# Order on VectorE, larger output-projection chunks, a second issuer for the first weights, and another pace for attention's fill

## The chip, the cores and the metric

The kernel runs on one core of one Trainium2 chip, as one launch. The metric is device time in microseconds (us), the median of several runs. Five engines work side by side, each with its own queue of instructions: TensorE (PE; its weight loads are shown apart as PEld), VectorE (DVE), ScalarE (ACT), GpSimd (POOL) and SyncE (SP), which here issues nearly all DMAs. An instruction waits at the head of its engine's queue until its inputs and its buffer are there, and everything behind it waits too.

## The reference

One transformer block in float32 on 512 tokens with 1024 features, then a last norm (`reference`, cut):

```
x = x + 0.5 * swiglu(rmsnorm(x, norm_ffn1), w_gate1, w_up1, w_down1)     # 1024 -> 2816 -> 1024
x = x + hybrid_mixer(rmsnorm(x, norm_mix), w_in, ..., w_out, rel_bias)
x = x + 0.5 * swiglu(rmsnorm(x, norm_ffn2), w_gate2, w_up2, w_down2)
return rmsnorm(x, norm_final)
# hybrid_mixer: 8 "moba" heads (0 to 7) and 8 "nsa" heads (8 to 15) of 64 features;
# an nsa head sums three gated attentions: compressed keys, selected keys (ks), window keys (kw);
# the heads' outputs, side by side, are multiplied by w_out (1024 x 1024).
```

## The kernel before

**Precision.** Every float32 operand of a matmul is split into a high and a low half (`hi` by ScalarE, `lo = v - hi` by VectorE, or by GpSimd for weights during attention). A product is then three matmuls (`mm3`, L99 to L102): hi by hi, hi by lo, lo by hi. A matmul with 512 columns moves one 128x128 block against all tokens.

**Stages.** x lies transposed as eight blocks `xs[0..7]` of 128 features by 512 tokens. The stages are: loading x and the first weights (L110 to L121); the first feed-forward layer; the mixer (projections, attention, output projection); the second feed-forward layer; the last norm.

**Feed-forward (class `Ffn`).** The first four of the 22 blocks of hidden features are computed plainly (`plain`): a gate step and an up step each load a 512 KB chunk of weights and run 24 matmuls of 512 columns. The other eighteen are computed in pairs (`pair`) by a scheme with seven products in place of eight: a pair has 14 steps (seven products, each for gate and for up) of 12 matmuls of 256 columns. Four of the seven products, S1 to S4, take sums of weight blocks, which `sums` (L298 to L303) makes in place on VectorE, 144 in all; `halves_of` (L305 to L311) then splits a block into `sph` and `spl` with `halves_of_x` (L225). The weight blocks lie in 16 buffers `aw`, eight to a pair, and a later pair's DMA waits until its buffers are free. `down` multiplies by the down projection and adds to xs (L487). Between the plain steps and the first pairs, `sums_of_x` and `blocks_of_x` make the moving operands of the pairs on VectorE.

**What sets the order.** `go` (L424) writes the steps out in program order: at step i it emits loads for step i+12, sums for step i+6, splits for step i+4, the products of step i, and the evictions of step i-1. A planner then orders each engine's queue at compile time by its own estimate of times: an instruction whose inputs it takes to be ready may go ahead of one that stands earlier in the program. `tc.issue_after(ins)` keeps the instructions of its block, on the engine of `ins`, behind `ins`; `tc.high_priority()` moves some ahead. On the chip the order within a queue is fixed.

**Attention and its fill.** Attention (L1006 to L1032) is a list of steps: 52 for the nsa heads (13 for each of four pairs of heads), then 24 for the moba heads. A step is three parts, `logits` (matmuls, softmax), `turn` (transposes) and `values`. Between them runs the fill: jobs of `stream` (L780), each with a chunk of weights loaded and split three jobs ahead. The fill's jobs are, in order, the projections for the kw keys and for the next heads (24 matmuls of 512 columns, eight units of three), and parts of the output projection `w_out` (L766), whose jobs wait until the heads that they read are done (`out_done`). `target(i)` (L1021) says how many units are to have run at step i: 1.4 for each nsa step, 0.6 for each moba step. `need` runs fill at once when a step needs its result, and what is left runs after the last step.

**Output projection.** 32 jobs: for each of the eight output blocks d and each two of the eight input blocks k, a 128 KB DMA, two splits of 128x256, six matmuls into one of two PSUM banks `mm`, and an addition to xs[d] (L774). The jobs for k = 2, 3 (heads 4 to 7) come last; after each of them xs[d] is multiplied by the next norm's gain and split (`gained`, L143) and its squares are added up (`squares`, L157). A head's output is split in `out_halves` (L806): the last step adds two parts into `lo` on GpSimd (L823).

Of the kernel before, what the change touches and what calls it, by code (L numbers as in the profile page):

```python
# [29 lines left out]
def block_kernel(ctx: ExitStack, tc: tile.TileContext, A: dict, out: bass.AP):  # L30
# [81 lines left out]
    first_w = [chunk((8, 128)) for _ in range(2)]  # L112
    for k in range(NK):
        x = xp.tile([128, S], F32, name=f"x{k}")
        nc.sync.dma_start(x, A["xT"][k * 128:(k + 1) * 128])
        xs.append(x)
        if k == 0:
            nc.sync.dma_start(gcol, A["gcol"])
        if k < 4:
            i, h = k % 2, slice(4 * (k // 2), 4 * (k // 2) + 4)  # L120
            nc.sync.dma_start(first_w[i][:, h], A[("wg1", "wu1")[i]][0][:, h])  # L121
# [65 lines left out]
    class Ffn:  # L187
# [14 lines left out]
        def __init__(self, wg, wu, which, tmp, hp, sp):  # L202
            self.w, self.which, self.tmp, self.hp, self.sp = (wg, wu), which, tmp, hp, sp
            self.xg, self.hs, self.steps = None, {}, []
            self.b, self.temps = {}, {}
            self.behind_rms = None
# [18 lines left out]
        def halves_of_x(self, hi, lo, v):  # L225
            nc.scalar.activation(hi, v, AF.Copy)  # L226
            nc.vector.tensor_tensor(lo, v, f32(hi), ALU.subtract)  # L227
# [61 lines left out]
        def pair(self, f):  # L289
# [8 lines left out]
            def sums(m, name):  # L298
# [4 lines left out]
                nc.vector.tensor_tensor(to, x, y, op)  # L303
# [65 lines left out]
        def down(self, w, fs, then, tag="mm", groups=(1,) * NK):  # L369
# [9 lines left out]
            def halves_of(d):  # L379
                if d % (4 // n) == 0:  # L380
                    i = d * n % 8
                    for k, v in enumerate(halves(raw[d * n // 8][:, i:i + 4])):
# [72 lines left out]
    def bias_rows(hp):  # L455
# [5 lines left out]
        nc.sync.dma_start(tabs[0:32, :], A["rel_bias"])  # L461
        nc.sync.dma_start(far, A["rel_bias"][31:32, :].to_broadcast([32, 16]))
        rows = hp.tile([16, RVW], F32, name="rows", tag="h", bufs=16)
        parts = []
        for src, h0, c, m in ((A["oh_t"], 0, 0, RVW), (A["oh_c"], 8, 0, S), (A["oh_c"], 8, S, S)):
            oh = hp.tile([33, S], F32, name="oh", tag="h", bufs=16)
            nc.sync.dma_start(oh[:, :m], src[:, c:c + m])
# [83 lines left out]
    with ExitStack() as ph:  # L551
# [214 lines left out]
        def w_out(d, k0, k1):  # L766
            def body(w):
                while any(2 * k + 1 not in out_done for k in range(k0, k1)):
                    yield
                p = pt("mm", "pw")  # L770
                for k in range(k0, k1):
                    mm3(p, w[k - k0], oT[k], k == k0, k == k1 - 1)
                    yield
                nc.vector.tensor_tensor(xs[d], p, xs[d], ALU.add)  # L774
                if k1 == 4:
                    got["x", d] = gained(d, 2)
                    squares(tmp, d, "t", 6)
            return A["w_o"][d][:, k0:k1], body
# [27 lines left out]
        def out_halves(h):  # L806
# [16 lines left out]
            nc.gpsimd.tensor_tensor(lo[b], t[b], u[b], ALU.add)  # L823
# [146 lines left out]
        for i in range(4):  # L970
            fill += [proj(2 * i, moba_t("q", i)), proj(2 * i + 1, moba_t("k", i))]
            if i == 2:
                fill += [w_out(d, 4, 6) for d in range(NK)]
        fill += [w_out(d, k, k + 2) for k in (6, 0) for d in range(NK)]
        last = [w_out(d, 2, 4) for d in range(NK)]
# [45 lines left out]
        def target(i):  # L1021
            if i < n_nsa:
                return 1.4 * i
# [118 lines left out]
def _laid_out(x, norm_ffn1, w_ffn1_gate, w_ffn1_up, w_ffn1_down, norm_mix, w_in, cmp_pos_k, cmp_w1_k,  # L1142
# [22 lines left out]
        "w_o": _blocks(w_out[0], D, 128),  # L1165
# [29 lines left out]
```

## Time and profile before

| | us |
|---|---|
| median of three runs | 1010.56 |
| the three runs | 1010.56, 1012.22, 1008.08 |
| the profiled execution, device time | 1011.25 |
| its span, first to last instruction | 1009.5 |

| engine | busy us | share of the span |
|---|---|---|
| PE | 983.8 | 97% |
| PEld | 871.0 | 86% |
| DVE | 776.9 | 77% |
| ACT | 564.9 | 56% |
| POOL | 137.3 | 14% |

The span is one profiled execution; device time is the span and what lies around it (1.75 us). Matmuls are pipelined: the next one starts before the shown end of the one before, so the shares of PE count a little more than its work. The moment at which a matmul starts, and the idle time ahead of it, are exact enough to be read.

By time, the first feed-forward layer lies at 0 to about 400 us, the projections at 400 to 440, attention with its fill at 440 to 636, the end of the output projection at 636 to 654, the second feed-forward layer from 648 to the end.

### The profile page before, as it was taken

To read this page: it belongs to the slowest core of one execution; us is meant where nothing else is said; L and a number is where in the kernel's file an instruction comes from. 1 tells how busy PE (TensorE), PEld (TensorE's weight loads), DVE (VectorE), ACT (ScalarE), POOL (GpSimd) and SP (SyncE) were. 2 spreads that over 40 slices of the span, in tenths; PEclk is the share of its full clock that TensorE was granted. 3 is DMA by queue.
4 is the path that set the end of the run, shared out by engine and by line. 5 is a ranking of instruction groups with operands and counts; after the bars stand their busy time and mean duration, and the time that the engine had idled before them with its cause. 6 is when DMAs were issued, how large, how long until landed. Compare 5 with 4: busy or idle time off the path is not lost.

```text
span 1009.5 us, 17013 instructions
## 1 busy us (share of the span) xinstructions
PE 983.8 (97%) x6080; PEld 871.0 (86%) x6080; DVE 776.9 (77%) x1578; ACT 564.9 (56%) x1181; POOL 137.3 (14%) x193
## 2 busy tenths in 40 slices
PE   8999999999999999999999999999999999999996
PEld 6779999999999898787878888788899999999995
DVE  6797888788766488758888978779878888776744
ACT  6463654454444266557677977655455445444436
POOL 0000000000000000036555776300000000000002
PEclk9999999999999999999999999999999999999998
DMA  7254544233501125541011322425244232341102
GB/s 244 87 197 153 186 149 113 98 101 89 161 25 54 45 85 177 165 127 38 20 45 32 93 65 84 140 86 209 69 144 142 86 105 91 120 146 43 33 11 84
DMA packets 53513, 104.53 MB, mean 104 GB/s; under 512 B 10513, under 2 KB 19170, under 8 KB 53428
## 3 DMA queue, kind: packets, MB, share of 16 engines
q1 hardware_dynamic: 53428, 103.44, 32.6%
q8 instruction: 48, 0.79, 0.3%
q14 instruction: 37, 0.30, 0.1%
HBM read 97.98 MB, written 5.30 MB: 102 GB/s over the span
## 4 chain that ended last, share of the span: by engine, by line
PE 82%; DVE 11%; DMA 3%; issue 2%; ACT 1%; POOL 0%; SPq 0%; DVEq 0%; ACTq 0%; POOLq 0%
PE pd L102 6%; PE pd L100 6%; PE pd L101 6%; PE pu L100 6%; PE pu L102 5%; PE pu L101 5%; PE pw L100 4%; PE pw L101 4%; PE pw L102 4%; PE pp L102 3%; PE pgu L100 3%; PE pp L100 3%; PE pp L101 3%; PE pgu L101 3%; PE pv L100 3%; PE pgu L102 3%
## 5 line engine op out<-in xcount | busy, mean ns | idle before, releaser
L226 ACT ACTIVATE sph<-aw 128x512 fp32r<-128x512 f32 x252 | 155.7, 628 | 138.0 <-PE pu L101 68.1
L91 ACT ACTIVATE whi<-raw 128x512 fp32r<-128x512 f32 (+2 forms) x216 | 124.6, 589 | 151.3 <-PE pd L101 71.8
L227 DVE TENSOR_TENSOR spl<-aw,sph 128x512 fp32r<-128x512 f32 x252 | 170.0, 685 | 49.5 <-ACT sph L226 47.9
L101 PE MATMUL pd<-h,whi 128*128 128x512 f32 x336 | 131.9, 392 | 1.4 <-DVE h L255 1.4
L102 PE MATMUL pd<-h,wlo 128*128 128x512 f32 x336 | 130.9, 390 | 0.8 <-DVE wlo L95 0.6
L95 DVE TENSOR_TENSOR wlo<-raw,whi 128x512 fp32r<-128x512 f32 (+1 forms) x168 | 110.9, 671 | 23.9 <-ACT whi L91 22.6
L100 PE MATMUL pd<-h,whi 128*128 128x512 f32 x336 | 129.0, 392 | 0.0
L100 PE MATMUL pu<-th,sph 128*128 128x256 f32 x432 | 121.5, 281 | 1.1 <-DVE t L339 1.1
L303 DVE TENSOR_TENSOR aw<-aw 128x512 f32<-128x512 f32 x144 | 97.6, 683 | 31.7 <-DMA aw<-in_wg 13.6
L102 PE MATMUL pu<-th,spl 128*128 128x256 f32 x432 | 121.1, 280 | 0.0
L101 PE MATMUL pu<-tl,sph 128*128 128x256 f32 x432 | 121.0, 280 | 0.0
L487 DVE SCALAR_TENSOR_TENSOR x<-pd,x 128x512 f32<-128x512 f32 x88 | 59.9, 685 | 44.7 <-PE pd L102 44.4
L100 PEld LDWEIGHTS pu<-th,sph 128*128 128x128 f32 x432 | 81.6, 189 | 2.8 <-DVE t L339 1.3
L101 PEld LDWEIGHTS pu<-tl,sph 128*128 128x128 f32 x432 | 81.9, 190 | 1.1
L100 PE MATMUL pw<-xo,sph 128*128 128x256 f32 x288 | 80.8, 281 | 0.8 <-DVE x L487 0.5
L102 PEld LDWEIGHTS pu<-th,spl 128*128 128x128 f32 x432 | 81.2, 188 | 0.1
L101 PE MATMUL pw<-xo,sph 128*128 128x256 f32 x288 | 80.4, 280 | 0.0
L102 PE MATMUL pw<-xo,spl 128*128 128x256 f32 x288 | 79.7, 280 | 0.0
L102 PEld LDWEIGHTS pd<-h,wlo 128*128 128x128 f32 x336 | 63.1, 188 | 14.1 <-DVE wlo L95 1.2
L101 PEld LDWEIGHTS pd<-h,whi 128*128 128x128 f32 x336 | 63.3, 188 | 12.8 <-DVE h L255 2.2
L100 PEld LDWEIGHTS pd<-h,whi 128*128 128x128 f32 x336 | 62.9, 188 | 11.1
L100 PEld LDWEIGHTS pw<-xo,sph 128*128 128x128 f32 x288 | 54.1, 188 | 2.6 <-ACT sph L226 1.6
(245 smaller groups left out, 2454.5 us busy)
## 6 DMA issues: line engine op xcount, KB each, us to landing
aw<-in_wg SPq DMA_DIRECT2D x72, 256.0 KB, 3.8
aw<-in_wu SPq DMA_DIRECT2D x72, 256.0 KB, 3.6
raw<-in_wd1a SPq DMA_DIRECT2D x20, 512.0 KB, 4.7
raw<-in_wd2a SPq DMA_DIRECT2D x20, 512.0 KB, 4.8
raw<-in_w_a SPq DMA_DIRECT2D x16, 512.0 KB, 4.4
raw<-in_w SPq DMA_DIRECT2D x8, 512.0 KB, 3.7
raw<-in_w_o SPq DMA_DIRECT2D x32, 128.0 KB, 2.2
raw<-in_wg SPq DMA_DIRECT2D x7, 512.0 KB, 3.8
```

Of the source, the lines that this page charges most:

```text
L91: nc.scalar.activation(hi, v, AF.Copy)
L95: nc.vector.tensor_tensor(lo, v, f32(hi), ALU.subtract)
L100: nc.tensor.matmul(p, w[0], v[0], start=first, stop=False, skip_group_check=again)
L101: nc.tensor.matmul(p, w[0], v[1], start=False, stop=False, skip_group_check=again)
L102: nc.tensor.matmul(p, w[1], v[0], start=False, stop=last, skip_group_check=again)
L226: nc.scalar.activation(hi, v, AF.Copy)
L227: nc.vector.tensor_tensor(lo, v, f32(hi), ALU.subtract)
L303: nc.vector.tensor_tensor(to, x, y, op)
L487: nc.vector.scalar_tensor_tensor(xs[d], p, 0.5, xs[d], ALU.mult, ALU.add)
```

## The change

It makes six edits. (1) Each sum of weights, and each split of down-projection weights, is kept on VectorE behind the newest `lo` of `halves_of_x` that the program has written so far (`behind_lo`). (2) The first gate weights are issued by ScalarE as two halves ahead of x; the first up weights come from SyncE as one DMA behind x; the small loads for the bias are kept behind them. (3) The output projection has eight jobs of four output blocks and two input blocks, a 512 KB DMA each; the last two jobs run k outside and the four blocks inside, in four banks (two `mm`, two `s`). (4) `lo` of head 7 is added on VectorE. (5) `target` begins at 8 and rises by 1.4 - 8/52 = 1.246 for each nsa step, with the same value at step 52. (6) The layout of w_out in memory follows (3).

```diff
     first_w = [chunk((8, 128)) for _ in range(2)]
+    for h in (slice(0, 4), slice(4, 8)):
+        nc.scalar.dma_start(first_w[0][:, h], A["wg1"][0][:, h])
     for k in range(NK):
         x = xp.tile([128, S], F32, name=f"x{k}")
         nc.sync.dma_start(x, A["xT"][k * 128:(k + 1) * 128])
         xs.append(x)
         if k == 0:
             nc.sync.dma_start(gcol, A["gcol"])
-        if k < 4:
-            i, h = k % 2, slice(4 * (k // 2), 4 * (k // 2) + 4)
-            nc.sync.dma_start(first_w[i][:, h], A[("wg1", "wu1")[i]][0][:, h])
+    fetch(first_w[1], A["wu1"][0])
...
         def halves_of_x(self, hi, lo, v):
             nc.scalar.activation(hi, v, AF.Copy)
-            nc.vector.tensor_tensor(lo, v, f32(hi), ALU.subtract)
+            self.last_lo = nc.vector.tensor_tensor(lo, v, f32(hi), ALU.subtract)
+
+        def behind_lo(self):
+
+            return tc.issue_after(self.last_lo.ins) if self.last_lo else nullcontext()
...
-                nc.vector.tensor_tensor(to, x, y, op)
+                with self.behind_lo():
+                    nc.vector.tensor_tensor(to, x, y, op)
...
-                    for k, v in enumerate(halves(raw[d * n // 8][:, i:i + 4])):
+                    with self.behind_lo():
+                        parts = halves(raw[d * n // 8][:, i:i + 4])
+                    for k, v in enumerate(parts):
                         got[d + k // n, k % n] = v
...
-        nc.sync.dma_start(tabs[0:32, :], A["rel_bias"])
-        nc.sync.dma_start(far, A["rel_bias"][31:32, :].to_broadcast([32, 16]))
+        with behind_fetched():
+            nc.sync.dma_start(tabs[0:32, :], A["rel_bias"])
+            nc.sync.dma_start(far, A["rel_bias"][31:32, :].to_broadcast([32, 16]))
...
-        def w_out(d, k0, k1):
+        def w_out(g, k0, last=False):
+
             def body(w):
-                while any(2 * k + 1 not in out_done for k in range(k0, k1)):
+                while any(2 * k + 1 not in out_done for k in (k0, k0 + 1)):
                     yield
-                p = pt("mm", "pw")
-                for k in range(k0, k1):
-                    mm3(p, w[k - k0], oT[k], k == k0, k == k1 - 1)
+                ps = {}
+                for i, k in [(i, k) for k in range(2) for i in range(4)] if last else [
+                        (i, k) for i in range(4) for k in range(2)]:
+                    if k == 0:
+                        ps[i] = pt("mm" if not last or i < 2 else "s", "pw")
+                    mm3(ps[i], w[2 * i + k], oT[k0 + k], k == 0, k == 1)
                     yield
-                nc.vector.tensor_tensor(xs[d], p, xs[d], ALU.add)
-                if k1 == 4:
-                    got["x", d] = gained(d, 2)
-                    squares(tmp, d, "t", 6)
-            return A["w_o"][d][:, k0:k1], body
+                    if k == 1:
+                        d = 4 * g + i
+                        nc.vector.tensor_tensor(xs[d], ps[i], xs[d], ALU.add)
+                        if last:
+                            got["x", d] = gained(d, 2)
+                            squares(tmp, d, "t", 6)
+            return A["w_o"][k0 // 2, g], body
...
-            nc.gpsimd.tensor_tensor(lo[b], t[b], u[b], ALU.add)
+
+            (nc.vector if h == 7 else nc.gpsimd).tensor_tensor(lo[b], t[b], u[b], ALU.add)
...
-                fill += [w_out(d, 4, 6) for d in range(NK)]
-        fill += [w_out(d, k, k + 2) for k in (6, 0) for d in range(NK)]
-        last = [w_out(d, 2, 4) for d in range(NK)]
+                fill += [w_out(g, 4) for g in range(2)]
+        fill += [w_out(g, k) for k in (6, 0) for g in range(2)]
+        last = [w_out(g, 2, True) for g in range(2)]
...
         def target(i):
             if i < n_nsa:
-                return 1.4 * i
+                return 8 + (1.4 - 8 / n_nsa) * i
             return 1.4 * n_nsa + 0.6 * (i - n_nsa)
```

## Rows read from the trace of the kernel before

**Rows 1.** Page, busy us of each engine, share of the span, instructions
```profile
PE 983.8 (97%) x6080; PEld 871.0 (86%) x6080; DVE 776.9 (77%) x1578; ACT 564.9 (56%) x1181; POOL 137.3 (14%) x193
```

**Rows 2.** Windows: stretch, length, busy us (instructions) by engine, granted clock, DMA, GB/s
```profile
48.00:104.00 56.00, 53.37 (x315) 46.38 (x314) 50.94 (x96) 28.33 (x59) 0.00 (x0) 1.00 0.49 170
690.00:765.00 75.00, 72.33 (x487) 65.58 (x486) 63.99 (x118) 40.96 (x84) 0.00 (x0) 1.00 0.40 135
104.00:400.00 296.00, 295.61 (x2007) 273.32 (x2006) 223.25 (x395) 150.99 (x294) 1.41 (x5) 1.00 0.34 105
...
457.00:478.00 21.00, 18.56 (x116) 14.75 (x115) 17.99 (x71) 16.27 (x47) 11.31 (x18) 1.00 0.13 37
504.00:518.00 14.00, 13.32 (x87) 10.55 (x85) 11.00 (x36) 11.78 (x31) 7.98 (x12) 1.00 0.07 19
636.00:650.00 14.00, 11.60 (x50) 8.61 (x50) 10.41 (x16) 10.49 (x20) 4.28 (x5) 1.00 0.51 160
```

**Rows 3.** Timeline of SP, ACT and PE at 0 to 7: start, us, work [idle <-releaser]
```profile
1.65 0.43 SPq L121 DMA_DIRECT2D raw<-in_wg  x1
...
3.76 0.72 ACT L147 ACTIVATE xo<-x,gcol 128x512 fp32r<-128x512 f32 x1 [1.53 <-DMA gcol<-in_gcol]
5.71 0.63 ACT L91 ACTIVATE whi<-raw 128x512 fp32r<-128x512 f32 x1 [1.23 <-DMA raw<-in_wg]
...
6.39 0.79 PE L100 MATMUL pgu<-xo,whi 128*128 128x512 f32 x1 [1.15 <-ACT whi L91]
```

**Rows 4.** Windows of the start, columns as in rows 2
```profile
6.40:11.00 4.60, 4.60 (x10) 2.85 (x11) 3.19 (x5) 3.24 (x6) 0.00 (x0) 1.00 0.99 338
11.00:25.00 14.00, 14.00 (x63) 11.57 (x62) 12.48 (x21) 10.48 (x19) 0.00 (x0) 1.00 0.75 238
```

**Rows 5.** Timeline of DVE: three moments at 61 to 97, one at 757
```profile
61.20 0.67 DVE L303 TENSOR_TENSOR aw<-aw 128x512 f32<-128x512 f32 x1
...
67.96 0.67 DVE L255 TENSOR_TENSOR h<-t,h 128x512 fp32r<-128x512 f32 x1
...
96.14 0.69 DVE L303 TENSOR_TENSOR aw<-aw 128x512 f32<-128x512 f32 x1 [1.88 <-DMA aw<-in_wg]
...
757.16 0.69 DVE L303 TENSOR_TENSOR aw<-aw 128x512 f32<-128x512 f32 x1 [4.23 <-DMA aw<-in_wg]
```

**Rows 6.** Windows of the projections' tile pp alone: PE, PEld, DVE
```profile
457.00:478.00 21.00, 0.24 (x2) 0.31 (x3) 0.67 (x1) 1.00 0.13 37
478.00:504.00 26.00, 17.99 (x72) 12.98 (x70) 1.28 (x2) 1.00 0.06 17
```

**Rows 7.** Waits of PE at 430 to 660: us in total, times, longest
```profile
PE pw L101 <- POOL kvn L823: 1.6, 1, 1.6
...
PE pw L100 <- DVE x L774: 0.8, 2, 0.5
```

**Rows 8.** Timeline of DVE and POOL at the end of the output projection
```profile
637.01 0.68 DVE L820 TENSOR_TENSOR to<-po,kvn 64x512 f32<-64x512 f32 x1 [0.41 <-POOL wlo L93]
...
638.46 1.26 POOL L823 TENSOR_TENSOR kvn<-to,u 64x512 fp32r<-64x512 f32 x1 [1.49 <-ACT u L822]
...
649.01 0.74 DVE L148 SCALAR_TENSOR_TENSOR xo<-x,gcol,xo 128x512 fp32r<-128x512 f32 x1
649.67 0.68 DVE L774 TENSOR_TENSOR x<-pw,x 128x512 f32<-128x512 f32 x1
650.27 0.67 DVE L164 TENSOR_TENSOR acc<-acc,sq 128x512 f32<-128x512 f32 x1
```

**Rows 9.** Groups by shape at 430 to 660: count, busy us, mean ns, idle before
```profile
L91 ACT ACTIVATE whi<-raw 128x512 fp32r<-128x512 f32 x27 | 16.9, 627 | 10.7 <-PE pp L101 6.4 <-issue 1.8 <-ACT th L891 0.8
L91 ACT ACTIVATE whi<-raw 128x256 fp32r<-128x256 f32 x32 | 13.2, 414 | 12.6 <-PE pw L101 7.0 <-PE pp L101 3.8 <-POOL kvn L823 0.9
L93 POOL TENSOR_TENSOR wlo<-raw,whi 128x256 fp32r<-128x256 f32 x32 | 24.8, 780 | 10.6 <-ACT whi L91 9.1 <-PE pw L101 1.1
L93 POOL TENSOR_TENSOR wlo<-raw,whi 128x512 fp32r<-128x512 f32 x16 | 21.2, 1324 | 4.0 <-ACT whi L91 4.0
```

More of the change, by code (lines that the diff above doesn't have):

```diff
@@ L205, in __init__ @@
             self.b, self.temps = {}, {}
+            self.last_lo = None
             self.behind_rms = None
@@ L466, in bias_rows @@
             oh = hp.tile([33, S], F32, name="oh", tag="h", bufs=16)
-            nc.sync.dma_start(oh[:, :m], src[:, c:c + m])
+            with behind_fetched():
+                nc.sync.dma_start(oh[:, :m], src[:, c:c + m])
             parts.append((oh, h0, c, m))
@@ L1164, in _laid_out @@
         "pos": c(cat([pos, pos], axis=0)),
-        "w_o": _blocks(w_out[0], D, 128),
+        "w_o": c(w_out[0].reshape(4, 2, 128, 2, 4, 128).transpose(0, 3, 2, 4, 1, 5)).reshape(4, 2, 128, 8, 128),
         "wg2": _blocks(w_ffn2_gate[0], D, 128), "wu2": _blocks(w_ffn2_up[0], D, 128),
```

## The prediction

> **What bounds the kernel now.** I read the page first. TensorE is busy for 983.8 of 1009.5 us, 97% [rows 1], and the change takes no matmul away and adds none: the same products of the output projection come in another order. So the ceiling on any gain is TensorE's idle time, 1009.5 - 983.8 = 25.7 us, and each edit can win only what lies idle where it acts. That is why I read the windows next, stretch by stretch. The long stretches of pairs are full: at 104 to 400 TensorE idles for 296.00 - 295.61 = 0.39 us [rows 2]. The idle time that the edits can reach lies in short places: the change from plain steps to pairs in each feed-forward layer (56.00 - 53.37 = 2.63 at 48 to 104, 75.00 - 72.33 = 2.67 at 690 to 765), attention's stretches without fill (2.44 at 457 to 478, 0.68 at 504 to 518, and one more of 0.65 like it at 535 to 548), and the end of the output projection (14.00 - 11.60 = 2.40 at 636 to 650) [rows 2]; to these comes the start, where the first product waits 1.15 us [rows 3]. Together 12.6 us. The waits and the timelines then say what ended each. (The profiled execution took 1011.25 us, its span 1009.5 and 1.75 around it; the median of the runs is 1010.56. I take the sum off the median; off the profiled execution it would come 0.7 later. A difference under 0.5%, 5.05 us, counts as no change, so faster means under 1005.5 and slower over 1015.6.)
>
> **The change, part by part.**
>
> *First weights by ScalarE.* ScalarE splits x's first block at 3.76, when the gains have landed, then sits idle for 1.23 us until the first half of the gate's weights lands, splits it in 0.63 at 5.71, and the first product starts at 6.39 [rows 3]. The weights were third in SyncE's queue, issued at 1.65. Issued by ScalarE at the outset, they are there when x is: split of x to 3.76 + 0.72 = 4.48, split of the weights to 5.11, so the first product at about 5.25, when the eight warming matmuls end (6.39 less its idle 1.15). That is 1.1 earlier. The trace has no DMA issued by ScalarE; SyncE's took 0.43, so two take 0.86 ahead of a ScalarE that idles 1.53 before 3.76 [rows 3]: hidden at that price, and up to 0.76 each. What is late next: the up weights now come behind x, as the last 512 KB. With the DMA engines 99% busy at 338 GB/s [rows 4], these two 256 KB take 2 x 0.78 = 1.6 us. The first products run at 4.60/10 = 0.46 us each, later ones at 14.00/63 = 0.222, both with a granted clock of 1.00 [rows 4]; 24 gate products from 5.25, the slow pace held to 11, last until about 13.5, and the up weights should be split about 0.2 later. I take -0.9. Bounds: -1.6, if the fast pace comes earlier too, and +1.6, if the up weights keep TensorE waiting for their whole landing.
> The Trainium skill (DMA: Bandwidth & Descriptors, "Issuing engines are not separate DMA queues") says that DMAs from ScalarE and SyncE share the same 16 engines, and a second issuer saves the issue time alone. Taken alone it makes this edit worth the two issues, 0.86 instead of 0.9, so nothing hangs on it here. The 99% of [rows 4] agrees that the engines, not the issuer, are then the limit.
>
> *Sums behind the newest lo.* At 48 to 104 VectorE is busy for 50.94 of 56.00 [rows 2]. Sums for the coming pairs go ahead of work needed sooner: the first at 61.20, three more before `h` at 67.96 [rows 5], which TensorE's down products wait for. At 96.14 a sum sat 1.88 us at the head of the queue until its DMA landed, with an eviction behind it that TensorE needed; at 757.16 another sat 4.23 [rows 5]. Held behind the newest `lo`, four sums of 0.67 leave the path of `h` (2.7 us), so the early half of these stalls should go; what is late next is the sums themselves, in a stretch where VectorE has only 5 us free. A sum that waits for its DMA is not cured by order: its buffer came free late, so its stall shrinks only as far as the splits before it come earlier. I take 60% of 2.63 + 2.67 = 5.30: -3.2. Bounds: -5.3 (all of it) and +3 (the four sums now hold a product back instead). In the long stretches the 144 sums gain nothing, with 0.39 us idle; what they could lose is a rival below. Splits of down weights under the same rule: nothing, since a down step's weights are split four steps ahead of their use, and a step is 12 products at 295.61/2007 = 0.147 us [rows 2], 1.8 us.
>
> *Attention's fill.* At 457 to 478 two matmuls of projections ran, at 478 to 504 seventy-two [rows 6]; in the first stretch VectorE is busy for 17.99 of 21.00 and TensorE idles for 2.44 [rows 2]. Before, 18.2 units (1.4 x 13) are due at the end of the first pair of heads; after, 8 + 1.246 x 13 = 24.2. Six units, 18 matmuls x 0.222 = 4.0 us, move into that stretch, from work that otherwise runs where TensorE is full. They can fill 2.44 at most, for the chain through VectorE needs TensorE at moments of its own: I take -2.0. Each later pair gets 1.246 x 13 = 16.2 units instead of 18.2, and the stretches with 0.68 and 0.65 idle stay. Bounds: -2.4, and +2.7: four units (8 less the 4.2 due at step 3) are put ahead of the first heads and push their chain back by 12 x 0.222.
>
> *Output projection in fours, and head 7 on VectorE.* TensorE's one long wait after attention is 1.6 us for `lo` of the last head [rows 7], which GpSimd made in 1.26 from 638.46 [rows 8]. Now the last job runs k = 2 for four blocks first, 12 products x 0.222 = 2.7 us that need no head but the earlier ones, and the addition takes about 0.68 on VectorE (a row of the same shape [rows 8]) in place of 1.26. The wait is gone: -1.6. Two waits for a bank, 0.8 together [rows 7], meet four banks in place of two: -0.5. Against it: four evictions now come within 3 x 0.67 us, each with 0.68 + 0.74 + 0.67 = 2.1 us of VectorE behind it [rows 8]. If VectorE takes them strictly in turn, the fourth bank is free 3 x 2.1 + 0.7 = 7.0 us after the first block is done, and TensorE wants it after 2 x 3 x 0.67 = 4.0: a stall of 3.0, which products of the next layer can cover, as far as they are planned there. I take -2.1; bounds -2.4 and +0.9. The splits: 32 of 128x256 become 16 of 128x512, so ScalarE saves 13.2 - 16 x 0.627 = 3.2 us and GpSimd 24.8 - 16 x 1.324 = 3.6 [rows 9]; neither ends a wait of TensorE here, so zero. A chunk's split is longer (1.32 for 0.78), but it is covered by the 24 products, 5.3 us, of the chunk before it. SyncE issues eight DMAs for 32: zero, the queue stands waiting for buffers.
>
> The sum: -0.9 - 3.2 - 2.0 - 2.1 = -8.2, so 1010.56 - 8.2 = **1002.4 us**. The bounds add up to -11.7 and +8.2, 998.9 to 1018.8; that all lie at one end is unlikely. The planner lays out every queue anew, so a wait can also vanish or appear elsewhere, a few us either way; and TensorE's pace loses time that the idle column does not count. For both I let the low end go to 995.
>
> **The rivals.**
> *A. Only the certain parts hold.* VectorE bounds the change to pairs whatever the order, and the fill finds no idle moment. Then the start and the end are left: -0.9 - 2.1 = -3.0, 1007.6, no change. For it: VectorE is busy for 91% of 48 to 104. Against: at 690 to 765 it has 11.0 us free [rows 2].
> *B. Sums come late in every pair; slower.* A sum behind a `lo` that waits for ScalarE or a buffer can itself be late for its product. Place: the products S1 to S4 of eighteen pairs, 144 of them. Price: at 0.1 us each 14.4; with the other parts, -5.0, it gives 1010.56 - 5.0 + 14.4 = 1020. It decides from (5.05 + 5.0)/144 = 0.07 us a sum on. For it: TensorE has no slack there. Against: the order that is forced is about that of the program, where a sum stands two steps (3.5 us) ahead of its split and six ahead of its product, and VectorE has 296.00 - 223.25 = 72.8 us free at 104 to 400 [rows 2].
> *C. The fill moves the stall.* Eight units ahead push the heads' chain by 2.7 us, and thinner fill later opens the 0.68 and 0.65 by as much again as they are: -0.9 - 3.2 - 2.1 + 2.7 + 1.3 = -2.2, 1008.4, no change. For it: the stretch at 457 to 478 is VectorE's. Against: VectorE idles ahead of it, so the chain can start later at no cost.
>
> **How the numbers follow.** Forecast 0.58, A 0.18, C 0.12, B 0.12. The forecast's own range is 997 to 1006; nearly all of it, 0.55, and some of A and C, 0.07, are faster by over 0.5%: 0.62. Slower: most of B, 0.10, and a rest of the others, 0.01: 0.11. Within 0.5%: 0.27. The range 995 to 1012 leaves out B and a thin low end.
>
> **What would show it.** Start: the first `pgu` product near 5.25. Sums: no `aw` sum on VectorE between 61 and 68 ahead of `h`, and TensorE's idle time in the two changes to pairs down from 5.3 to about 2. Fill: matmuls of `pp` or `pw` in the stretch of the first pair's end, TensorE's idle time there under 0.5. End: no wait of `pw` for `kvn`. The prediction is wrong if TensorE waits for S1 to S4 in the long stretches (B), if the four banks wait for VectorE by over 1 us, or if TensorE's busy time, not its idle time, moves.

## The result: slower by 0.67%, and the profile after

The changed kernel takes 1015.83 us (median of 6 runs, 1014.07 to 1020.39), the kernel before on the same chip 1010.35 (6 runs). The ratio is 1.0067, with an interval from 1.0050 to 1.0085. It is slower by 5.5 us where 8.2 us were to be gained, and it lies outside the range. The profiled execution took 1015.73 us, its span 1013.9.

The page of the kernel after, busy time by engine:

```profile
PE 986.0 (97%) x6080; PEld 875.6 (86%) x6080; DVE 781.9 (77%) x1579; ACT 564.5 (56%) x1165; POOL 132.4 (13%) x176
```

TensorE runs the same 6080 matmuls and is busy for 2.2 us more than in [rows 1]; the rest of the 4.4 us by which the span grew is idle time. Its waits, of the whole execution (us in total, times, longest), name three places that were to get better:

```profile
PE pd L101 <- DVE h L260: 4.0, 2, 2.1
PE pr L175 <- DVE acc L164: 2.0, 1, 2.0
PE pgu L100 <- ACT whi L91: 1.9, 1, 1.9
```

Windows of the kernel after, columns as in [rows 2]:

```profile
15.70:21.30 5.60, 4.53 (x12) 3.29 (x13) 5.26 (x9) 2.67 (x6) 0.00 (x0) 0.70 0.38 121
108.00:404.00 296.00, 296.00 (x2008) 273.97 (x2007) 229.81 (x404) 154.85 (x297) 1.40 (x5) 1.00 0.35 106
464.90:485.90 21.00, 18.47 (x97) 15.06 (x96) 16.54 (x59) 14.67 (x39) 8.93 (x14) 0.76 0.12 38
475.20:485.40 10.20, 9.01 (x33) 6.85 (x34) 7.14 (x25) 6.44 (x17) 4.76 (x7) 0.50 0.03 5
638.00:652.00 14.00, 14.00 (x64) 11.43 (x63) 11.55 (x20) 9.03 (x18) 2.54 (x2) 1.00 0.22 76
664.00:670.00 6.00, 4.74 (x18) 3.95 (x19) 1.38 (x4) 1.36 (x2) 0.00 (x0) 0.72 0.34 87
```

The reader is to see three things. The long stretch of pairs stays full, 296.00 of 296.00. The end of the output projection is full now, 14.00 of 14.00 where [rows 2] has 11.60. And in three stretches the granted clock is below 1.00: 0.70 from 15.7 on, 0.50 (1.2 GHz, the lower of its two levels) for the ten us from 475.2, 0.72 from 664. At 16 and at 665 TensorE had just stood for 1.9 and 2.0 us; ahead of 475.2 the heads' products ran alone, with waits of 0.48, 0.61 and 0.24 in 3.6 us.

Where the time went is seen best when TensorE's products are counted through both traces, each by its columns (256 at least): for each moment of the trace before, the moment at which the changed kernel has done as much. Its lag in us:

| at (us, before) | 20 | 52 | 68 | 160 | 440 | 490 | 630 | 650 | 670 | 705 | 720 | 800 | 985 |
|---|---|---|---|---|---|---|---|---|---|---|---|---|---|
| lag of the kernel after | +4.4 | +4.1 | +6.4 | +1.6 | +0.2 | +3.1 | +5.0 | +1.9 | +5.7 | +8.0 | +6.2 | +4.1 | +4.1 |

So 4.1 is lost at the start, 2.2 at the first change to pairs, 4.8 in attention, 3.8 behind the output projection and 2.4 at the second change to pairs. Gains lie between: 4.8 in the pairs after the first change (68 to 160), 3.1 at the end of the output projection (630 to 650), 4.0 after the second change. The 1.4 at 160 to 440 is a stretch at the lower clock that the trace before has (0.51 from 413.50 to 416.90) and the one after has not.

**The start.** Timeline of ScalarE and TensorE in the kernel after (start, us, work, idle before):

```profile
12.04 3.73 ACT L163 ACTIVATE sq<-x 128x512 f32<-128x512 f32 x7
15.68 2.70 ACT L91 ACTIVATE whi<-raw 128x512 fp32r<-128x512 f32 x5
...
16.35 0.50 PE L100 MATMUL pgu<-xo,whi 128*128 128x512 f32 x1 [1.94 <-ACT whi L91]
```

The up weights' split stands behind the squares of x in ScalarE's queue. TensorE waits 1.94 us for it.

**The change to pairs.** Timeline of VectorE in the kernel after, cut to sums, splits and `h`:

```profile
65.19 1.29 DVE L228 TENSOR_TENSOR spl<-aw,sph 128x512 fp32r<-128x512 f32 x2
66.39 0.68 DVE L309 TENSOR_TENSOR aw<-aw 128x512 f32<-128x512 f32 x1
66.99 0.68 DVE L228 TENSOR_TENSOR spl<-aw,sph 128x512 fp32r<-128x512 f32 x1
67.59 0.68 DVE L309 TENSOR_TENSOR aw<-aw 128x512 f32<-128x512 f32 x1
...
68.80 0.68 DVE L228 TENSOR_TENSOR spl<-aw,sph 128x512 fp32r<-128x512 f32 x1
...
70.07 0.68 DVE L260 TENSOR_TENSOR h<-t,h 128x512 fp32r<-128x512 f32 x1
```

Two sums have left the path of `h`, as the edit says. Four splits of pair weights have come in their place, and `h` starts at 70.07 where [rows 5] has 67.96. Measured against TensorE, which is 4.1 us behind here, `h` is not late; TensorE waits for it nevertheless, because its own queue has another order as well. In the kernel before, 50 products of this down projection run ahead of the first one that needs the low half of `h`; in the kernel after, 34 do. Windows of its tile pd on TensorE, from its first product to that one, in the kernel before and the kernel after:

```profile
56.80:68.60 11.80, 11.49 (x50) 1.00 0.64 242
```

```profile
60.90:70.70 9.80, 7.87 (x34) 1.00 0.65 246
```

**Attention.** Windows of the tile pp alone in the kernel after (PE, PEld, DVE), the counterparts of [rows 6]:

```profile
464.90:485.90 21.00, 0.15 (x1) 0.00 (x0) 0.67 (x1) 0.76 0.12 38
485.90:511.90 26.00, 11.76 (x48) 8.86 (x48) 0.67 (x1) 1.00 0.15 47
```

The stretch without fill was moved by 8 us, not filled: one matmul in 21.00 us, where there were two.

### The profile page after: what moved, and what is told of

Read it like the earlier page. It is cut to its first block, busy times and chain, and to the rows that moved or that the text cites. A ratio compares the mean times of both kernels' runs of the same rounds, so it can differ in the third digit from the quotient of the medians.

```text
span 1013.9 us, 16889 instructions
## 1 busy us (share of the span) xinstructions
PE 986.0 (97%) x6080; PEld 875.6 (86%) x6080; DVE 781.9 (77%) x1579; ACT 564.5 (56%) x1165; POOL 132.4 (13%) x176
## 4 chain that ended last, share of the span: by engine, by line
PE 84%; DVE 7%; DMA 4%; ACT 2%; issue 2%; SPq 1%; ACTq 0%; DVEq 0%
PE pd L101 7%; PE pd L102 7%; PE pd L100 7%; PE pu L101 7%; PE pu L102 7%; PE pu L100 7%; PE pw L100 5%; PE pw L102 4%; PE pw L101 4%; PE pp L102 3%; PE pp L100 3%; PE pp L101 3%; PE pv L100 3%; PE pv L101 3%; PE pv L102 3%; PE ps_t L905 2%
## 5 line engine op out<-in xcount | busy, mean ns | idle before, releaser
L227 ACT ACTIVATE sph<-aw 128x512 fp32r<-128x512 f32 x252 | 157.9, 630 | 168.3 <-PE pu L101 91.0
L91 ACT ACTIVATE whi<-raw 128x512 fp32r<-128x512 f32 (+1 forms) x200 | 121.8, 621 | 177.5 <-PE pd L101 88.4
```

## The experiments

My theory after this reading: no edit costs by its own work. Each moves an instruction that TensorE needs behind others in a queue (or, in attention, leaves a stretch without products), and the wait costs a second time where the granted clock falls behind it. The rival: the edits themselves take time, VectorE's order in the long pairs above all. Every ratio is against the kernel before on the same chip; "lag" is meant as in the table. A lag comes from one profiled execution of each kernel, and chance is in it: five of the kernels below (the target alone, the output projection alone, the sum of squares later, the hold, target and hold) run the instructions of TensorE, VectorE and ScalarE in the order of the kernel before up to 400 us, and yet their lags at 160 lie between -0.6 and +2.5. Readings of one or two us rest on the ratios, or on several traces that agree.

### Each edit alone

**The start alone.** 

> The kernel before with the start's edit alone (ScalarE issues the first gate weights, up weights behind x). Theory: in the changed kernel the up weights' split stands behind the eight squares of x in ScalarE's queue, TensorE idles 1.9 us for it and then runs 3.4 us at half clock, so that the first layer's last plain product ends 4.1 us later; alone it should do the same: that moment at about 60.7 instead of 56.6, and the whole kernel about +4 us. Rival (my prediction): -0.9 us, with the moment near 55.7. Second rival: the loss comes only from the planner's other reordering; then this kernel is within 1 us of before at that moment.

```diff
+    for h in (slice(0, 4), slice(4, 8)):
+        nc.scalar.dma_start(first_w[0][:, h], A["wg1"][0][:, h])
...
+    fetch(first_w[1], A["wu1"][0])
```

1011.37 us, ratio 1.0027 [1.0009, 1.0045]. TensorE's largest wait is the one for the up weights' split:

```profile
PE pgu L100 <- ACT whi L91: 3.0, 1, 3.0
```

The lag at 52 is +4.5, like the changed kernel's. The start's loss is this edit's own.

**VectorE's order alone.** 

> The kernel before with VectorE's order alone (sums and down splits behind the newest lo). Theory: it is the part that works: each change from plain steps to pairs shrinks, by 2.4 us in the first layer and 1.6 in the second as in the changed kernel; whole kernel -4.0 us. Rival B of the prediction (sums late for their products in the long stretches): slower than before, TensorE's idle time at 104 to 400 well above 0.4 us. Third: no change, since VectorE bounds those places whatever its order.

```diff
-                nc.vector.tensor_tensor(to, x, y, op)
+                with self.behind_lo():
+                    nc.vector.tensor_tensor(to, x, y, op)
```

1011.75 us, ratio 1.0024 [1.0007, 1.0042]. Its largest group of waits:

```profile
PE pd L101 <- DVE h L260: 6.5, 2, 4.2
```

In the kernel before, the wait at this first place is 0.3 us. VectorE and TensorE in this run, and below them a split and the wait in the kernel before:

```profile
68.99 0.67 DVE L260 TENSOR_TENSOR h<-t,h 128x512 fp32r<-128x512 f32 x1
69.72 0.79 PE L101 MATMUL pd<-h,whi 128*128 128x512 f32 x1 [4.19 <-DVE h L260]
70.27 1.27 DVE L95 TENSOR_TENSOR wlo<-raw,whi 128x512 fp32r<-128x512 f32 x2
```

```profile
62.47 0.67 DVE L95 TENSOR_TENSOR wlo<-raw,whi 128x512 fp32r<-128x512 f32 x1
PE pd L101 <- DVE h L255: 0.3, 1, 0.3
```

`h` starts 1.03 us later than before (68.99 for 67.96). The rest of the new wait comes from TensorE's side: from 65.5 on the product that needs `h` is at the head of its queue, after 34 products of the down projection where there were 50. Splits of weights into `wlo` have moved behind `h` too: VectorE ran one at 62.47 before and has none here between 58.2 and 70.27, and six of the sixteen products read a `wlo`. Whether the sums or the splits of down weights moved the sixteen was not run apart. From 68 to 76 the granted clock is 0.57. The lag goes to +5.7 at 96, falls to +3.1 at 160, rises by 2.6 at 705, where again sixteen products fewer stand ahead of the wait, and falls by 3.9 until 800. The gain of 4.0 us that was expected was missed. The long stretches lose nothing, so rival B of the prediction is refuted.

**The output projection alone.** 

> The kernel before with the output projection in fours, its layout, and head 7's lo on VectorE. Theory: the wait for the last head goes (-2.8 us of idle time at 636 to 650), but the first finished x block comes some 5 us later, VectorE's chain of gain and squares ends later, and the sum over features (pr) holds TensorE for about 2 us, with a half clock of 3.4 us behind it (1.7 us): about +1 us as a whole. Rival: it is also what slowed attention by 4.8 us in the changed kernel (other splits, other DMAs); then +5 us or more, with the last po product about 641 instead of 636.

```diff
-            return A["w_o"][d][:, k0:k1], body
+            return A["w_o"][k0 // 2, g], body
...
+            (nc.vector if h == 7 else nc.gpsimd).tensor_tensor(lo[b], t[b], u[b], ALU.add)
```

1009.78 us, ratio 1.0000 [0.9985, 1.0015]. The lag goes from +0.3 at 630 to -2.8 at 655: 3.1 gained. Then TensorE waits 2.0 us for the sum of squares (`pr` for `acc`), the clock falls, and at 670 the lag is +1.0. VectorE in the kernel after, which has the same wait (the last addition that it waits for is at 664.52):

```profile
661.74 1.41 DVE L164 TENSOR_TENSOR acc<-acc,sq 128x512 f32<-128x512 f32 x2
663.31 1.29 DVE L95 TENSOR_TENSOR wlo<-raw,whi 128x512 fp32r<-128x512 f32 x2 [0.15 <-PE pgu L102]
664.52 0.68 DVE L164 TENSOR_TENSOR acc<-acc,sq 128x512 f32<-128x512 f32 x1
```

ScalarE had finished the last square at 656.76; its addition stands in VectorE's queue behind splits of the next weights. The gain and the new wait are one edit's two sides.

**The fill's target alone.** 

> The kernel before with attention's fill evened alone (target from 8 at step 0). Theory: this is what slowed attention: one more projection runs ahead, the stretch without fill stays 21 us long, and TensorE falls to half clock in it; the last po product at about 641 instead of 636, whole kernel +4 to +5 us. Rival (my prediction): -2.0 us. Second rival: attention's loss came with the output projection's chunks; then this one is within 1 us of before.

```diff
-                return 1.4 * i
+                return 8 + (1.4 - 8 / n_nsa) * i
```

1013.41 us, ratio 1.0052 [1.0034, 1.0070]. The lag grows by 4.2 between 440 and 630, as in the changed kernel (4.8). The window of pp alone shows the moved stretch again:

```profile
464.00:485.00 21.00, 0.73 (x4) 0.26 (x2) 0.67 (x1) 0.92 0.07 19
```

Alone the four edits add up to 1.03%, together they lost 0.67%. They are not independent: where the start is late, `h` is waited for 2.0 us instead of 4.2.

**Everything but the fill's target.** 

> The changed kernel with the target of the fill as before. Theory (the fill edit alone lost attention's 4.75 us and the 10.2 us of half clock at 475; the other edits lose as they do alone): attention gives back 3.5 to 4.5 us, the waits at 16, 70, 665 and 711 stay, 1011 to 1012 with before at 1008 to 1009, ratio 1.002 to 1.0035. Rival (attention's loss came from the later start of the heads or from the other edits' shift of buffers, not from the target): ratio 1.006 to 1.008 as with everything.

```diff
-                return 8 + (1.4 - 8 / n_nsa) * i
+                return 1.4 * i
```

1015.20 us (4 runs), ratio 1.0050 [1.0032, 1.0068]. Attention loses 0.6 between 440 and 630 instead of 4.8, as the theory has it. But the whole time came out between the two expectations, and its interval overlaps that of the changed kernel: in its profile the start was 1.3 us later still, and the stretch at the lower clock near 413 was back. Attention's loss is the target's; how much of the 0.67% that is cannot be told from these two times.

### What is behind the waits

**The squares put behind the up weights' split.** 

> The start's edit alone (as e1_start), with the squares of x put behind the first up weights' split on ScalarE and VectorE. Theory (queue order): TensorE's 3.04 us wait for that split goes down to what the landing of the up weights leaves, under 1 us, the half clock behind it goes too, and the last plain product ends at 56 to 57 instead of 61.2; whole kernel 4 us under e1_start at that moment. Rival (the up weights land too late, since 256 KB more go ahead of them): the wait stays at 2 us or more.

```diff
-                with tc.issue_after(made[0].ins):
+                with tc.issue_after(first_up[0].ins), tc.issue_after(first_up[1].ins):
```

This is the start alone, with ScalarE's and VectorE's squares held behind the two splits of the first up weights. 1007.57 us, ratio 0.9987 [0.9978, 0.9997]. ScalarE's timeline:

```profile
12.62 1.15 ACT L92 ACTIVATE whi<-raw 128x512 fp32r<-128x512 f32 x2 [1.15 <-DMA raw<-in_wu]
...
14.19 3.75 ACT L164 ACTIVATE sq<-x 128x512 f32<-128x512 f32 x7
```

The weights are there at 12.62, 3.06 us before the split in the changed kernel, and the lag at 52 is -0.7. So the loss was the place in the queue, not the landing. Once mended, the edit is worth about what was forecast: 0.7 us by the lag, 1.3 (0.3 to 2.2) by the ratio.

**TensorE kept at work in the wait.** 

> The start's edit alone, with 13 matmuls of ones into an unused bank put between the first gate's last product and the first up product, so that TensorE is busy in the 3.04 us in which it waits there; nothing else is changed and the up products cannot start earlier. Theory (the half clock follows TensorE's idle time): the granted clock stays 1.0 from 15 to 22 and the last plain product ends 2.5 to 3.4 us earlier than in e1_start, near 58. Rival (the half clock comes whatever TensorE did, or from the dense work before it): no change, 61.2.

```diff
+                    with tc.issue_after(last_mm[0].ins):
+                        for _ in range(13):
+                            last_mm[0] = nc.tensor.matmul(wake.rearrange("p (a b) -> p a b", a=4), ones,
+                                                          ones.unsqueeze(1).to_broadcast([128, 4, 128]),
+                                                          start=True, stop=True)
```

The start alone, with 13 matmuls of ones in the place of the wait; they add nothing to any output. 1010.01 us, ratio 1.0023 [1.0010, 1.0036]. Two windows, first the start alone, then with the matmuls of ones:

```profile
14.00:22.00 8.00, 5.85 (x13) 4.16 (x14) 6.62 (x11) 4.51 (x9) 0.00 (x0) 0.57 0.51 162
```

```profile
14.00:22.00 8.00, 7.47 (x32) 5.57 (x31) 6.89 (x11) 4.46 (x9) 0.00 (x0) 1.00 0.56 166
```

The granted clock is 1.00 instead of 0.57, and the last plain product comes 2.2 us earlier (58.94 for 61.17), a little less than expected, although the same split is waited for. So the lower clock came from TensorE's standing still, and it held 2.2 of the 4.5 us. That is a reading of the two profiles; the ratios, 1.0023 and 1.0027, are too close to tell the two kernels apart.

**`h`'s low half by GpSimd.** 

> VectorE's order alone (as e2_sums), with the low half of the last plain block's h made by GpSimd, which is idle there, instead of VectorE. Theory: in e2_sums TensorE waits 4.19 us at 65.5 because that one instruction stands behind four splits and two sums in VectorE's queue; out of that queue it is ready at about 66, TensorE waits under 1 us, no half clock follows, and the first layer's pairs end 3 to 5 us earlier than in e2_sums (349.7). Rival (VectorE bounds that stretch whatever the order): the wait only moves to the next operand, the down weights' splits, and the pairs end within 1.5 us of e2_sums.

```diff
-            nc.vector.tensor_tensor(lo, h, f32(hi), ALU.subtract)
+            (nc.gpsimd if f == FP - 1 else nc.vector).tensor_tensor(lo, h, f32(hi), ALU.subtract)
```

This was to take `h` out of VectorE's queue, on top of the order alone. It missed: 1016.41 us (4 runs), ratio 1.0081 [1.0063, 1.0099]. GpSimd's timeline says why:

```profile
64.47 8.08 POOL L260 TENSOR_TENSOR h<-t,h 128x512 fp32r<-128x512 f32 x1 [63.16 <-ACT h L259]
```

One subtraction took 8.08 us; GpSimd's 128x512 splits in attention take 1.324 each [rows 9]. TensorE's wait for `h` grew from 4.2 to 7.2 us, and no more can be read from it.

**The sum of squares under the next gate products.** 

> The output projection alone (as e3_wout), with the sum over features of the second layer's norm allowed 24 products later (ahead of the second up chunk instead of the second gate chunk). Theory: in e3_wout TensorE waits 2.1 us for that sum at 660 because VectorE's chain behind the four-block job ends late, and then runs 3.4 us at half clock; with 24 products (5.4 us) to cover it, both go: end of the plain products 3 to 4 us earlier than in e3_wout (696.1), whole kernel 3 us faster than before. Rival: the chain is late anyway and what follows needs the norm at once; then the wait moves behind the 24 products and nothing is won.

```diff
-        ffn.behind_rms = 1, 0
+        ffn.behind_rms = 1, 1
```

On top of the output projection alone, the up products of the second block, not its gate products, wait for the sum. 1008.87 us, ratio 0.9999 [0.9987, 1.0011]. The wait of `pr` is gone, and 655 to 695 lose nothing (lag -1.6 throughout, where the output projection alone went from -2.8 to +1.0). Still the whole kernel wins nothing, as the rival has it. In the profile 2.6 are lost between 720 and 740. It would be natural to say that the gain was given back at VectorE's next full stretch, but that is not shown: the start alone, whose output projection is that of before, loses 2.4 there too. The profiled execution was also the slowest of its ten runs (1011.31).

**The order from the second pair on.** 

> The kernel before with the VectorE order alone, but in force only from the second pair of blocks on: ahead of the first products of the down projection the order of VectorE's queue is that of before, four sums and then h. Theory (the order is good wherever h is not waited for; the 4.19 us wait and the half clock behind it were the whole loss of the order in force everywhere): no wait of pd for h beyond what before has, progress within 0.5 us of before at 96 us, then the 2.5 us by 160 and the 4 us of the second network's pairs are gained, so 4 to 6 us under before, ratio 0.994 to 0.996. Rival (the later gains were only the delay caught up again: with products late, VectorE ran ahead of them): ratio 0.9985 to 1.0015, and the progress curve stays within 1 us of before from 96 to 200 and from 705 to 800.

```diff
+            return tc.issue_after(self.last_lo.ins) if self.last_lo and self.at >= 4 * FP + 14 else nullcontext()
```

1007.78 us (12 runs), ratio 0.9980 [0.9967, 0.9992]. Ahead of `h` the queue is that of before, and no new wait is there (lag -0.1 from 25 to 96). The kernel is 2.0 us faster (0.8 to 3.3), between the two expectations. In the profile it gains 1.2 from 96 to 160 and 1.7 between 720 and 800, less than the order alone won back at those places, 2.7 and 3.9. How much of this is the order's cannot be read from lags: the squares put behind the split, whose second layer runs in the order of before, also gain 1.0 between 720 and 800. And delay is caught up again without the order: the start alone, 4.4 late at 96, is 2.6 late at 160. So the order alone's later gains were in part delay caught up, as the rival has it, and a small gain is the order's own, by the ratio.

**The fill's products held.** 

> The kernel before with one thing more: during the first eight heads each unit of fill has its products held in TensorE's queue behind the heads' instruction issued three calls earlier, so that they cannot be pulled forward. In the order of TensorE's queue the lumps of 19 to 24 matmuls with stretches of none between them become threes spread over all of the steps. Theory (rival C of the prediction: the fill loses time because it runs ahead in lumps and leaves stretches empty; it is the lumps, not the heads' chain, that cost): the stretch 457 to 478 is filled, the 5.8 us that TensorE loses between 460 and 480 fall under 2.5, the half clock at 413.5 or near 475 is absent, last po 3 to 5 us earlier, ratio 0.995 to 0.997. Rival (the heads' chain of VectorE and ScalarE sets the pace of that stretch, and products put between its steps only lengthen it): last po within 1 us of before or later, ratio 0.999 to 1.004.

```diff
-                    mm3(p, w[k], xg[k], k == 0, k == NK - 1)
+                    with held():
+                        mm3(p, w[k], xg[k], k == 0, k == NK - 1)
...
+                hold[0] = heads[-3] if len(heads) >= 3 and i < n_nsa else None
                 run(max(0, int(target(i + (j + 1) / 3)) - done[0]))
```

`held()` is an `issue_after` on `hold[0]`, and `heads` collects the last matmul of each call of the heads. The planner cannot pull a product of the fill forward by more than three calls. 1008.27 us (12 runs), ratio 0.9983 [0.9971, 0.9994]. Windows of this kernel:

```profile
432.00:448.00 16.00, 11.76 (x60) 8.75 (x58) 9.97 (x26) 9.09 (x20) 2.41 (x4) 0.89 0.31 90
457.00:478.00 21.00, 20.40 (x119) 17.37 (x118) 17.56 (x60) 15.83 (x42) 11.72 (x17) 1.00 0.15 42
```

The stretch 457 to 478 is filled, 20.40 of 21.00. But the first heads now lack the fill that had run ahead: 4.24 idle at 432 to 448 (2.3 of it one wait for a DMA), a lag of +7.5 at 450, caught up by 620. So the stretch could be filled, and what was missing is at the beginning. The ratio of 0.995 to 0.997 that was expected was missed.

**Target and hold together.** 

> The kernel before with the fill edit of the change (target eight units ahead) and, from the fourth step of the heads on, each unit's products held behind the heads' instruction issued three calls earlier. It is the run of the target alone plus the hold, and the run of the hold alone plus the eight units at the beginning. Theory (eight units at the beginning are what the heads' first steps lack when the fill is held, 436 to 447 in the run of the hold; the target alone lost because nothing held the products): the 7.4 us that the held run lost between 430 and 460 fall under 3, the stretch 460 to 480 stays filled, last po 4 to 6 us before that of before, ratio 0.994 to 0.9965. Rival (eight units ahead push the heads' chain back whether held or not, as in the run of the target alone): last po at or behind that of before, ratio 1.000 to 1.005.

```diff
-                return 1.4 * i
+                return 8 + (1.4 - 8 / n_nsa) * i
...
+                hold[0] = heads[-3] if len(heads) >= 3 and 4 <= i < n_nsa else None
```

999.35 us (6 runs), ratio 0.9900 [0.9881, 0.9919]. The same target that lost 0.52% alone gains 1.0% when the products are held, more than the 0.35 to 0.6% that were expected. (Against the hold alone two things differ: the target, and the hold's beginning at the fourth step.) From 440 to 645 the lag goes from +1.3 to -9.6. Windows of the tile pp alone, twenty us each: first the kernel before, then this one.

```profile
440.00:460.00 20.00, 13.95 (x56) 10.34 (x56) 0.67 (x1) 1.00 0.38 108
460.00:480.00 20.00, 2.24 (x10) 1.99 (x11) 0.67 (x1) 1.00 0.05 14
480.00:500.00 20.00, 12.47 (x49) 8.69 (x48) 1.28 (x2) 1.00 0.07 20
500.00:520.00 20.00, 5.37 (x22) 4.31 (x23) 1.28 (x2) 1.00 0.05 14
```

```profile
440.00:460.00 20.00, 10.23 (x38) 6.28 (x36) 0.69 (x1) 1.00 0.33 92
460.00:480.00 20.00, 9.50 (x34) 5.91 (x33) 1.36 (x2) 1.00 0.13 41
480.00:500.00 20.00, 9.71 (x35) 6.41 (x36) 0.67 (x1) 1.00 0.08 21
500.00:520.00 20.00, 10.51 (x38) 6.13 (x37) 1.35 (x2) 1.00 0.17 41
```

56, 10, 49 and 22 matmuls have become 38, 34, 35 and 38. What that does to attention as a whole, again the kernel before and then this one:

```profile
440.00:647.00 207.00, 199.79 (x1117) 167.01 (x1117) 165.25 (x488) 153.10 (x386) 128.86 (x174) 1.00 0.22 64
```

```profile
440.00:637.00 197.00, 195.54 (x1122) 167.65 (x1121) 165.16 (x489) 151.61 (x386) 127.16 (x174) 1.00 0.24 66
```

Idle time falls from 207.00 - 199.79 = 7.2 us to 1.5. TensorE's busy time falls as well, by 4.3 us, for 1122 matmuls against 1117. So what is shown as busy between the heads' products had held time that was no work.

**The repaired parts together.** 

> What the runs point to, together: the start with the squares behind the up weights' split, the VectorE order from the second pair on, the fill's target of the change with its products held from the fourth step on, and the output projection of before. Theory (the three repairs act in different stretches and add): start 0.6 us earlier and no half clock there, 3 us from the order, 4 to 6 us in attention, ratio 0.990 to 0.994, 1000 to 1003.5 with before at 1009. Rival (they gain back the same slack, or a new half clock eats one): ratio 0.9955 to 0.999.

The edit is that of the squares behind the split, the order from the second pair on, and target and hold; the output projection is that of before. 995.64 us (5 runs), ratio 0.9870 [0.9855, 0.9886], faster than both kernels. The three ratios alone multiply to 0.9987 x 0.9980 x 0.9900 = 0.9867, so these parts do add, and the gain is larger than expected because attention's was. Its page:

```profile
PE 976.1 (98%) x6080; PEld 870.6 (88%) x6080; DVE 779.5 (78%) x1578; ACT 566.6 (57%) x1181; POOL 135.2 (14%) x193
```

The same 6080 matmuls, busy for 7.7 us less than in [rows 1], in a span of 993.9 that is 15.6 shorter.

## Why the prediction was wrong, step by step

- **Start, -0.9; measured +4.1.** The step that failed is "the up weights should be split about 0.2 later". I worked it out from the landing alone. The weights were there by 12.62 in the run with the squares behind, no later than I said; their split was behind squares in ScalarE's queue, whose 3.73 us I had left out. Even the bound, +1.6 for a wait until "their whole landing", was of the wrong kind. With the queue mended the edit gives -0.7 by the lag.
- **Sums, -3.2; measured +2.2 and +2.4 at `h`, with -4.8 and -4.0 after them, which are partly delay caught up.** The step that failed is "four sums of 0.67 leave the path of `h` (2.7 us)". With the order alone two sums left that path and four splits came, so that `h` started 1.03 us later instead of 2.7 earlier. And TensorE's queue, which the sum left out, was laid out anew: 34 products instead of 50 ahead of the one that needs `h`, and a wait of 4.19 us instead of 0.32. I had counted what leaves a queue, not what moves up in it, nor what changes in another engine's queue. Why the planner did so stays open. A sum bound to a `lo` may make that `lo` urgent to it; and splits of weights moved behind `h` as well (70.27 for 62.47), though I had put the splits of down weights at nothing. That the long stretches can carry the order was right. In force from the second pair on, where `h` is left alone, the order gains 2.0 us (0.8 to 3.3), so even there it is hardly the forecast's 3.2.
- **Fill, -2.0; measured +4.8.** Two steps failed. "Six units, 18 matmuls ... move into that stretch" is wrong: the target says when the program offers a unit, not when TensorE runs it, and [rows 6] had already shown lumps, 2 matmuls in one stretch and 72 in the next. The second is mis-sized: "They can fill 2.44 at most" took the idle time of one stretch as the ceiling. With the products held attention became about 10 us shorter, 5.7 of it idle time and 4.3 busy time. The place and the price of rival C, 2.7 + 1.3 = 4.0, were close to what happened; but that is luck: its mechanism, that eight units ahead push the heads' chain, is not borne out, since the same eight units gain when what follows them is held.
- **Output projection, -2.1; measured -3.1 and then +3.8.** The wait for the last head is gone, as forecast. The step that failed is that the bunched evictions are a stall "which products of the next layer can cover": they were covered from 649.5 to 662.9, and then `pr` waited 1.97 us for the sum of squares, whose last addition stood in VectorE's queue behind splits of weights, with the lower clock behind it. With that wait put off the kernel was still no faster, so what the edit is worth stays open.
- **What had no term at all: the clock.** The six runs of the changed kernel have a mean granted clock of 0.9895, the kernel before 0.996 in the runs beside the experiments. In work at full speed that is (0.996 - 0.9895) x 1014 = 6.6 us, about the whole loss. It is an upper bound, since a product that would wait anyhow loses nothing by it; the matmuls of ones took away one such stretch, and 2.2 us with it.
- **The ceiling.** "The ceiling on any gain is TensorE's idle time" and "each edit can win only what lies idle where it acts" are refuted as rules: in attention 10.0 us were won where 7.2 lay idle, and of the best version's 15.6 us, 7.7 came out of busy time. [rows 4] had shown it, 0.46 us a product at one place and 0.222 at another, both counted as busy.

What stays open: how the loss of 0.67% divides among the edits inside the changed kernel, since they overlap; which half of the order's edit changed TensorE's queue ahead of `h`; and whether the output projection in fours gains anything once VectorE has room at the next change to pairs. A version with all four edits mended was not tried.

## What to carry to other kernels

Before an instruction that the critical engine needs is moved or its data made to come earlier, list what stands ahead of it in its own engine's queue after the change: three of the four edits lost at this point. List also what the waiting engine still has to do ahead of the wait, for a planner may change that too: here 50 products became 34. Work that is to fill gaps is best bound to the gaps' own instructions, or a planner may run it in lumps, as this one did; the same target lost 0.5% free and gained 1.0% held. A new wait of TensorE can cost about twice its length: in the changed kernel the clock fell behind those at 16 and 665 us, not behind those of `h` at 70 and 711; and an evenly fed TensorE also sheds busy time, which the idle column doesn't show.

## What the hardware showed unexpectedly

GpSimd's subtraction of 128x512 took 8.08 us in the run with `h`'s low half by GpSimd, six times the 1.324 of such a subtraction in attention [rows 9]. It started at 64.47 and ended at 72.55. VectorE ran two-operand instructions without a gap until 71.42 and then stood still:

```profile
70.75 0.67 DVE L309 TENSOR_TENSOR aw<-aw 128x512 f32<-128x512 f32 x1
73.86 0.69 DVE L495 SCALAR_TENSOR_TENSOR x<-pd,x 128x512 f32<-128x512 f32 x1 [2.44 <-PE pd L102]
```

A second such subtraction, at 702.48 in the same run, took 7.46 and ended at 709.94, where VectorE had stopped at 708.82. So both ended 1.1 us after VectorE's unbroken run, which is nearly the time that the work takes by itself. VectorE's busy share alone does not explain it: it was 80% at 63 to 75 (9.56 of 12.00 us) and 80% in attention (165.25 of 207.00), where GpSimd took 1.324. The Trainium skill (GPSIMD Engine Reference, "Key points") says that GpSimd shares its SBUF interfaces with VectorE and contends with VectorE's instructions of two SBUF inputs; this trace agrees, and adds the size.
